# Eleven groups of one gate pair with right factors at an offset or read in steps, and matmuls in another order or size

## The chip, the cores and the metric

One core of a Trainium2 chip runs the whole kernel. The metric is the device time of one execution in microseconds (us), lower is better; of several runs the median is taken. The engines named below are PE (TensorE, matrix products; PEld are its weight loads), DVE (VectorE), ACT (ScalarE), POOL (GpSimd) and SP (SyncE, whose queue issues most transfers).

## The reference

One layer of a decoder on 512 tokens of 2048 channels, in float32: a norm and a projection `h @ w_in`; two mixers side by side on its columns (chunked gated linear attention with 4 heads, dilated sliding-window attention with 8 heads); `x + concat @ w_out`; then the feed-forward part

```
h2 = rms_norm(x, norm2_g[l])
x = x + (jax.nn.silu(h2 @ w_gate[l]) * (h2 @ w_up[l])) @ w_down[l]
```

with 5632 hidden columns. The change touches only `h2 @ w_gate` and `h2 @ w_up` for the hidden columns 2048 to 2559.

## The kernel before

All large products go through `pair` (L221 to L327). It computes two 512-column blocks of a product, `w1` and `w2`, by a Strassen-like scheme with seven products, in the order P1, P5, P6, P3, P7, P2, P4 (`PRODUCTS`, L32). A product runs over the groups `g` of 512 rows of the contracted side (four in a gate pair), and writes two accumulators `dst[m]` of 128 x 512 in PSUM, one bank each. For a group it takes the left combination `op.t[COMBO[prod], g]` (tiles AA and AS, made long before) and a right factor `src` of 128 x 2 x 512, which is a loaded quarter (a, b, c, d: tiles wa, wb, wc, wd; `load_quarter`, L215 to L219) or a difference of two quarters formed in place on DVE (L280, L283, L288, L293).

Float32 is carried in two parts in the matmul format `float32r`. ACT casts `src` to the high part wh (L295), DVE subtracts to get the low part wl (L297), and PE does 12 matmuls of 128 x 128 by 128 x 512 (L305): the high part with both parts of the left factor (eight), then the low part with its high part (four). The inner loop is

```
for w, terms in ((wh, (0, 1)), (wl, (0,))):
    for jj in range(2):
        for m in range(2):
            for hl in terms:
```

so that two matmuls in a row go to the same bank for wh, and every matmul changes bank for wl. wh and wl each have two buffers (`hpool`, L114), the quarters twelve (`wpool`, L113). After a group `step()` (L445) lets pieces of other work in: here, in the first groups of a gate pair, the transposes and stores of the pair before (L1014 to L1029) and the sums over its result (`sums_job`, L1305). When a product is complete its accumulators are copied to seeds by ACT (L243) or added to them by DVE (L255).

Eleven gate pairs (j = 0 to 10, L1348) run one after the other; the fifth has j = 4. Only the first `pair`-like function, `first_pair`, has its order of instructions on PE, ACT and DVE written by hand; after it the framework's planner orders the instructions of each engine when the program is built, gives out the buffers of a pool and adds the waits. P1.2 below is product P1, group 2 (groups count from 0).

Of the kernel before, what the change touches and what calls it, by code (L numbers as in the profile page):

```python
# [10 lines left out]
F32 = mybir.dt.float32  # L11
F32R = mybir.dt.float32r
U32 = mybir.dt.uint32
AF = mybir.ActivationFunctionType
ALU = mybir.AluOpType
# [3 lines left out]
P = 128  # L19
# [14 lines left out]
COMBO = {"P1": "A11", "P5": "S1", "P6": "S2", "P3": "S4", "P7": "S3", "P2": "A12", "P4": "A22"}  # L34
# [32 lines left out]
    "seedd",  # L67
    "closeb",
)
ON_VECTOR = "l1 u2 u4 u6 u7".split()  # L70


# [32 lines left out]
def block_kernel(ctx: ExitStack, tc: tile.TileContext, ins, out):  # L105
    nc = tc.nc
    x, w_in, w_out, w_gate, w_up, w_down = (
        ins[n] for n in ("x", "w_in", "w_out", "w_gate", "w_up", "w_down")
    )
# [3 lines left out]
    wpool = ctx.enter_context(tc.tile_pool(name="wpool", bufs=12))  # L113
    hpool = ctx.enter_context(tc.tile_pool(name="hpool", bufs=2))  # L114
# [10 lines left out]
    def nm(s):  # L125
        uid[0] += 1
        return f"{s}_{uid[0]}"
# [87 lines left out]
    def load_quarter(rows, name, g, w):  # L215
        r0 = rows[g][0 if name in "ab" else 1]
        t = wpool.tile([P, 2, 512], F32, name=nm("w" + name), tag="w")
        load(t, w[r0 : r0 + 256, :].rearrange("(j p) n -> p j n", p=P))
        return t  # L219

    def pair(op, rows, w1, w2, final, step, seed_scale=None):  # L221

        n = op.groups
        tt = nc.vector.tensor_tensor
        q = {}

        def quarter(name, g):
            if (name, g) not in q:
                q[name, g] = load_quarter(rows, name, g, w1 if name in "ac" else w2)
            return q[name, g]  # L230

        def accs():
            return [acc.tile([P, 512], F32, name=nm("acc"), tag="acc") for _ in range(2)]

        def seeds(src, half):
            res = []

            def one(m):
                t = cpool.tile([P, 512], F32, name=nm("seed"), tag="C")
                if seed_scale is None:  # L240
                    nc.scalar.copy(t, src[m])
                else:
                    nc.scalar.activation(t, src[m], AF.Copy, scale=seed_scale(half, m))  # L243
                res.append(t)

            later(1, lambda: one(0))
            later(2, lambda: one(1))
            return res

        def close(seed, src, half, which):  # L250
            def one(m):
                if seed_scale is None:
                    tt(seed[m], src[m], seed[m], op=ALU.add)
                else:
                    nc.vector.scalar_tensor_tensor(  # L255
                        seed[m], src[m], seed_scale(half, m), seed[m], op0=ALU.mult, op1=ALU.add
                    )
                if m == 1:
                    final(half, which, seed, None)

            later(1, lambda: one(0))
            later(2, lambda: one(1))

        X, Y, Z = None, None, None
        sa = sb = sc = None
        for prod in PRODUCTS:
            if prod == "P1":
                X = accs()
            elif prod == "P5":
                Y = accs()  # L270
            elif prod == "P2":
                Z = accs()
            dst = {"P1": X, "P5": Y, "P6": X, "P3": Y, "P7": X, "P2": Z, "P4": X}[prod]
            fresh = prod in ("P1", "P5", "P2")
            for g in range(n):
                if prod == "P1":
                    src = quarter("a", g)
                elif prod == "P5":
                    src = quarter("a", g)
                    tt(src, quarter("b", g), src, op=ALU.subtract)  # L280
                elif prod == "P6":
                    src = quarter("a", g)
                    tt(src, quarter("d", g), src, op=ALU.subtract)  # L283
                elif prod == "P3":
                    src = quarter("d", g)
                elif prod == "P7":
                    src = quarter("b", g)
                    tt(src, quarter("d", g), src, op=ALU.subtract)  # L288
                elif prod == "P2":
                    src = quarter("c", g)  # L290
                else:
                    src = quarter("a", g)
                    tt(src, quarter("c", g), src, op=ALU.subtract)  # L293
                wh = hpool.tile([P, 2, 512], F32R, name=nm("wh"), tag="wh")
                recent["act"] = nc.scalar.copy(wh, src).ins  # L295
                wl = hpool.tile([P, 2, 512], F32R, name=nm("wl"), tag="wl")
                tt(wl, src, wh.bitcast(F32), op=ALU.subtract)  # L297
                a = op.t[COMBO[prod], g]
                for w, terms in ((wh, (0, 1)), (wl, (0,))):
                    for jj in range(2):  # L300
                        for m in range(2):
                            for hl in terms:
                                first = g == 0 and w is wh and jj == 0 and hl == 0
                                last = g == n - 1 and w is wl and jj == 1
                                nc.tensor.matmul(  # L305
                                    dst[m],
                                    a[:, jj, hl, m * P : (m + 1) * P],
                                    w[:, jj, :],
                                    start=fresh and first,
                                    stop=last,  # L310
                                    skip_group_check=not fresh,
                                )
                step()
            if prod == "P1":
                sa = seeds(X, 0)
            elif prod == "P5":
                sb = seeds(Y, 1)
            elif prod == "P6":
                sc = seeds(X, 0)
            elif prod == "P3":  # L320
                close(sc, Y, 0, 1)
            elif prod == "P7":
                close(sb, X, 1, 1)
            elif prod == "P2":
                close(sa, Z, 0, 0)
            else:
                later(1, lambda: final(1, 0, None, X), hold=True)  # L327
# [113 lines left out]
    def later(units, fn, hold=False):  # L441

        deferred.append([units, fn, hold])

    def step(n=1):  # L445
        for d in list(deferred):
            d[0] -= 1
            if d[0] <= 0:
                deferred.remove(d)
                d[1]()  # L450
        if any(d[2] for d in deferred):
            return
        for _ in range(n):
            while background:
                try:
                    next(background[0])
                    break
                except StopIteration:
                    background.pop(0)
# [9 lines left out]
    def paced(counts):  # L469
        counts = iter(counts)  # L470
        return lambda: step(next(counts, 1))
# [113 lines left out]
    def x_turn(h, b, on_vector):  # L585
        bk = bank().rearrange("p (j n) -> p j n", j=2)
        for jj in range(2):
            for m in range(2):
                nc.tensor.transpose(
                    bk[:, jj, m * P : (m + 1) * P],  # L590
                    xt[h, b // 2][:, b % 2, m, jj * P : (jj + 1) * P],
                    ident,
                )
        dst = raw[b, h]
        if on_vector:
            nc.vector.tensor_tensor(
                dst, bk, g1[:, 2 * b : 2 * b + 2].unsqueeze(2).to_broadcast([P, 2, 256]), op=ALU.mult
            )
        else:
            for jj in range(2):  # L600
                nc.scalar.activation(
                    dst[:, jj, :], bk[:, jj, :], AF.Copy, scale=g1[:, 2 * b + jj : 2 * b + jj + 1]
                )
# [5 lines left out]
    for what in LOADS.split():  # L609
        name, i = what[0], int(what[1])  # L610
# [5 lines left out]
    for g in range(4):  # L616
        for b in (2 * g, 2 * g + 1):
            if g < 3:
                t = apool.tile([P, 2, 512], F32, name=nm("xT"), tag="A")
# [6 lines left out]
    def first_unit(what, *args):  # L626

        if what == "t":
            x_turn("ul".index(args[0][0]), int(args[0][1]), args[0] in ON_VECTOR)
            return  # L630
# [717 lines left out]
    for j in range(11):  # L1348
        c = slice(512 * j, 512 * j + 512)
        if j == 10:  # L1350
            background.append(down_jobs(0))
        pair(
            opn, rows_n, w_gate[:, c], w_up[:, c], final_ffn(j),
            paced(paces.get(j, ())), seed_scale=tok_scale,
        )


# [65 lines left out]
```

## Time and profile before

| | us |
|---|---|
| median of 3 runs (2046.26 to 2049.46) | 2046.87 |
| the profiled execution, its own time | 2051.18 |
| its span, first to last instruction | 2049.4 |
| PE busy | 2014.3 (98%) |
| DVE busy | 1659.6 (81%) |
| ACT busy | 1103.8 (54%) |

The page of the profile gives busy time by engine, the chain of work that ended last, and the costliest groups of instructions by line. Its times are those of one profiled execution, so a sum made from them stands against 2051.18 us, and the difference is then put on the median. A matmul's recorded duration is longer than the distance to the next one, since matmuls overlap; the pace is read from starts. Windows give busy times of a stretch, and the timeline gives instructions in order of time, neighbours of one kind merged ("x8").

### The profile page before, as it was taken

To read this page: it belongs to the slowest core of one execution; us is meant where nothing else is said; L and a number is where in the kernel's file an instruction comes from. 1 tells how busy PE (TensorE), PEld (TensorE's weight loads), DVE (VectorE), ACT (ScalarE), POOL (GpSimd) and SP (SyncE) were. 2 spreads that over 40 slices of the span, in tenths; PEclk is the share of its full clock that TensorE was granted. 3 is DMA by queue.
4 is the path that set the end of the run, shared out by engine and by line. 5 is a ranking of instruction groups with operands and counts; after the bars stand their busy time and mean duration, and the time that the engine had idled before them with its cause. 6 is when DMAs were issued, how large, how long until landed. Compare 5 with 4: busy or idle time off the path is not lost.

```text
span 2049.4 us, 25841 instructions
## 1 busy us (share of the span) xinstructions
PE 2014.3 (98%) x9226; PEld 1663.1 (81%) x9226; DVE 1659.6 (81%) x1850; ACT 1103.8 (54%) x1600; POOL 52.8 (3%) x81
## 2 busy tenths in 40 slices
PE   7999999999999999999999999999999999999999
PEld 6887888887777778888888888888888888888887
DVE  7996777768689789868868868778779979979977
ACT  7663564566666675544544445445446645545443
POOL 0000220011000000000000000000000000000000
PEclk9999999999999999999999999999999999999999
DMA  8347354454666685553554553553555855855662
GB/s 267 128 157 248 116 180 147 141 153 156 198 208 219 191 274 163 159 170 123 170 157 126 169 158 118 166 161 125 163 155 171 268 198 174 299 172 174 235 205 72
DMA packets 237114, 360.45 MB, mean 176 GB/s; under 512 B 18246, under 2 KB 96783, under 8 KB 236984
## 3 DMA queue, kind: packets, MB, share of 16 engines
q1 hardware_dynamic: 236776, 358.72, 55.5%
q8 instruction: 72, 1.18, 0.2%
q14 instruction: 58, 0.48, 0.1%
q10 hardware_dynamic: 208, 0.08, 0.0%
HBM read 296.59 MB, written 64.51 MB: 176 GB/s over the span
## 4 chain that ended last, share of the span: by engine, by line
PE 87%; DMA 5%; DVE 4%; issue 2%; ACT 1%; SPq 1%; POOL 0%; DVEq 0%; ACTq 0%; POOLq 0%
PE acc L305 79%; PE acc L373 3%; DVE wl L297 2%; PE bank L1014 1%; PE bank L921 1%; DMA wc<-in_w_in 1%; DMA xn_d<-oT 1%; PE bank L899 1%; DMA x<-in_x 1%; ACT wh L295 0%; DVE wa L283 0%; DMA r<-xn_d 0%; DVE AS L172 0%; PE bank L914 0%; PE bank L696 0%
## 5 line engine op out<-in xcount | busy, mean ns | idle before, releaser
L305 PE MATMUL acc<-wh,AS 128*128 128x512 f32 x3008 | 753.4, 392 | 3.6 <-ACT wh L295 2.2
L305 PEld LDWEIGHTS acc<-wh,AS 128*128 128x128 f32 x3008 | 563.5, 188 | 124.3 <-ACT wh L295 3.7
L295 ACT CAST wh<-wa 128x1024 fp32r<-128x1024 f32 x376 | 396.0, 1054 | 438.4 <-PE acc L305 382.4
L305 PE MATMUL acc<-wh,AA 128*128 128x512 f32 x2256 | 565.4, 393 | 0.0
L297 DVE TENSOR_TENSOR wl<-wa,wh 128x1024 fp32r<-128x1024 f32 x376 | 459.1, 1222 | 104.3 <-ACT wh L295 99.7
L305 PEld LDWEIGHTS acc<-wh,AA 128*128 128x128 f32 x2256 | 422.2, 188 | 87.7 <-issue 1.2
L305 PE MATMUL acc<-wl,AS 128*128 128x512 f32 x1504 | 403.8, 390 | 3.0 <-DVE wl L297 3.0
L305 PEld LDWEIGHTS acc<-wl,AS 128*128 128x128 f32 x1504 | 282.4, 188 | 63.7 <-DVE wl L297 5.3
L305 PE MATMUL acc<-wl,AA 128*128 128x512 f32 x1128 | 302.5, 390 | 1.5 <-DVE wl L297 1.3
L305 PEld LDWEIGHTS acc<-wl,AA 128*128 128x128 f32 x1128 | 211.4, 188 | 47.2 <-DVE wl L297 3.5
L295 ACT CAST wh<-wb 128x1024 fp32r<-128x1024 f32 x94 | 99.0, 1054 | 126.1 <-PE acc L305 122.8
L295 ACT CAST wh<-wc 128x1024 fp32r<-128x1024 f32 x94 | 98.9, 1053 | 123.2 <-PE acc L305 111.5
L295 ACT CAST wh<-wd 128x1024 fp32r<-128x1024 f32 x94 | 99.1, 1055 | 114.5 <-PE acc L305 114.5
L297 DVE TENSOR_TENSOR wl<-wd,wh 128x1024 fp32r<-128x1024 f32 x94 | 114.9, 1223 | 51.2 <-ACT wh L295 51.0
L297 DVE TENSOR_TENSOR wl<-wc,wh 128x1024 fp32r<-128x1024 f32 x94 | 114.9, 1223 | 50.5 <-ACT wh L295 50.1
L293 DVE TENSOR_TENSOR wa<-wc,wa 128x1024 f32<-128x1024 f32 x94 | 114.8, 1225 | 43.7 <-DMA wc<-in_w_gate 25.8
L297 DVE TENSOR_TENSOR wl<-wb,wh 128x1024 fp32r<-128x1024 f32 x94 | 114.6, 1221 | 9.6 <-ACT wh L295 9.3
L288 DVE TENSOR_TENSOR wb<-wd,wb 128x1024 f32<-128x1024 f32 x94 | 115.0, 1224 | 0.6
L283 DVE TENSOR_TENSOR wa<-wd,wa 128x1024 f32<-128x1024 f32 x94 | 114.3, 1222 | 0.2
L280 DVE TENSOR_TENSOR wa<-wb,wa 128x1024 f32<-128x1024 f32 x94 | 113.6, 1222 | 0.8
L255 DVE SCALAR_TENSOR_TENSOR seed<-acc,rs,seed 128x512 f32<-128x512 f32 x96 | 71.8, 748 | 30.9 <-PE acc L305 29.8
L243 ACT ACTIVATE seed<-acc,rs 128x512 f32<-128x512 f32 x96 | 60.8, 680 | 0.0
(286 smaller groups left out, 1370.6 us busy)
## 6 DMA issues: line engine op xcount, KB each, us to landing
wa<-in_w_gate SPq DMA_DIRECT2D x44, 512.0 KB, 4.2
wb<-in_w_up SPq DMA_DIRECT2D x44, 512.0 KB, 3.8
wd<-in_w_up SPq DMA_DIRECT2D x44, 512.0 KB, 4.0
wc<-in_w_gate SPq DMA_DIRECT2D x44, 512.0 KB, 3.6
wc<-in_w_in SPq DMA_DIRECT2D x28, 512.0 KB, 4.1
wa<-in_w_in SPq DMA_DIRECT2D x24, 512.0 KB, 4.9
wb<-in_w_in SPq DMA_DIRECT2D x24, 512.0 KB, 5.8
wd<-in_w_in SPq DMA_DIRECT2D x24, 512.0 KB, 5.9
```

The lines of the kernel that those rows point to most:

```text
L243: nc.scalar.activation(t, src[m], AF.Copy, scale=seed_scale(half, m))
L255: nc.vector.scalar_tensor_tensor(seed[m], src[m], seed_scale(half, m), seed[m], op0=ALU.mult, op1=ALU.add)
L280: tt(src, quarter("b", g), src, op=ALU.subtract)
L283: tt(src, quarter("d", g), src, op=ALU.subtract)
L288: tt(src, quarter("d", g), src, op=ALU.subtract)
L293: tt(src, quarter("c", g), src, op=ALU.subtract)
L295: recent["act"] = nc.scalar.copy(wh, src).ins
L297: tt(wl, src, wh.bitcast(F32), op=ALU.subtract)
L305: nc.tensor.matmul(dst[m], a[:, jj, hl, m * P : (m + 1) * P], w[:, jj, :], start=fresh and first, stop=last, skip_group_check=not fresh,)
L373: recent["pe"] = nc.tensor.matmul(dst[prod][m], a[:, jj, hl, m * P : (m + 1) * P], w[:, jj, :], start=fresh and g == 0 and len(terms) == 2 ...
L899: nc.tensor.matmul(lp[:, :n], qh[:, b * P : (b + 1) * P], kh[:, :n], start=True, stop=True)
L921: nc.tensor.matmul(op, vh[:, k, :], lgs[b][:, k * P : (k + 1) * P], start=(k == 0), stop=(k == b))
```

## The change

A table `FORMS` gives eleven groups of the pair j = 4 another form; `pair` gets it as an argument and, for these, calls the new `one_group` in place of its own cast, subtraction and matmuls.

- A number (P1.1: 1, P1.2: 4, P5.1: 8, P2.2: 16): the high part is cast, in two halves, into two tiles of the pool of the quarters, at an offset of so many elements. The low part is as before.
- `("read", b)` (P5.2: 2, P3.1: 4, P6.1: 16, P6.2: 256): both parts are written so that element k of a row comes to lie with its neighbour b elements further on, and are read back by the matmul with a step of b elements.
- `"same"` (P7.1): the high and the low right part follow each other on the same left factor.
- `"banks"` (P7.2): the matmuls change bank every time in the high part too.
- `"split"` (P2.1): each matmul becomes two of 256 columns.

In all eleven the low part is formed by two subtractions of 512 columns instead of one of 1024.

```diff
--- before.py
+++ after.py
@@ -67,6 +67,12 @@
     "seedd",
     "closeb",
 )
+
+FORMS = {
+    ("P1", 1): 1, ("P1", 2): 4, ("P5", 1): 8, ("P5", 2): ("read", 2), ("P6", 1): ("read", 16),
+    ("P6", 2): ("read", 256), ("P3", 1): ("read", 4), ("P7", 1): "same",
+    ("P7", 2): "banks", ("P2", 1): "split", ("P2", 2): 16,
+}
 ON_VECTOR = "l1 u2 u4 u6 u7".split()
 
 
@@ -218,7 +224,90 @@
         load(t, w[r0 : r0 + 256, :].rearrange("(j p) n -> p j n", p=P))
         return t
 
-    def pair(op, rows, w1, w2, final, step, seed_scale=None):
+    def spread(t, b):
+
+        return t.rearrange("p (a b) -> p b a", b=b)
+
+    def moving(form, src):
+
+        if isinstance(form, tuple):
+            b = form[1]
+            wh = hpool.tile([P, 2, 512], F32R, name=nm("wh"), tag="wh")
+            for jj in range(2):
+                nc.scalar.copy(
+                    spread(wh[:, jj], b), src[:, jj].rearrange("p (b a) -> p b a", b=b)
+                )
+            return [wh[:, 0], wh[:, 1]]
+        res = []
+        for jj in range(2):
+            t = wpool.tile([P, 2, 512], F32, name=nm("woff"), tag="w")
+            v = t.rearrange("p j n -> p (j n)").bitcast(F32R)[:, form : form + 512]
+            nc.scalar.copy(v, src[:, jj])
+            res.append(v)
+        return res
+
+    def one_group(form, src, dst, a):
+
+        tt = nc.vector.tensor_tensor
+
+        def mm(m, jj, hl, w, cols=None):
+            o, r = dst[m], w
+            if cols is not None:
+                o, r = o[:, cols], r[:, cols]
+            nc.tensor.matmul(
+                o, a[:, jj, hl, m * P : (m + 1) * P], r,
+                start=False, stop=False, skip_group_check=True,
+            )
+
+        def mv(m, jj, hl, w, o):
+            nc.tensor.matmul(
+                o, a[:, jj, hl, m * P : (m + 1) * P], w,
+                start=False, stop=False, skip_group_check=True,
+            )
+
+        if isinstance(form, (int, tuple)):
+            wh = moving(form, src)
+        else:
+            t = hpool.tile([P, 2, 512], F32R, name=nm("wh"), tag="wh")
+            nc.scalar.copy(t, src)
+            wh = [t[:, 0], t[:, 1]]
+        wl = hpool.tile([P, 2, 512], F32R, name=nm("wl"), tag="wl")
+        for jj in range(2):
+            if isinstance(form, tuple):
+                b = form[1]
+                o = spread(wl[:, jj], b)
+                x = src[:, jj].rearrange("p (b a) -> p b a", b=b)
+                y = spread(wh[jj].bitcast(F32), b)
+            else:
+                o, x, y = wl[:, jj], src[:, jj], wh[jj].bitcast(F32)
+            tt(o, x, y, op=ALU.subtract)
+        wl = [wl[:, 0], wl[:, 1]]
+        jm = [(jj, m) for jj in range(2) for m in range(2)]
+        if form == "same":
+            for jj, m in jm:
+                mm(m, jj, 0, wh[jj])
+                mm(m, jj, 0, wl[jj])
+            for jj, m in jm:
+                mm(m, jj, 1, wh[jj])
+            return
+        if form == "banks":
+            for w, terms in ((wh, (0, 1)), (wl, (0,))):
+                for hl in terms:
+                    for jj, m in jm:
+                        mm(m, jj, hl, w[jj])
+            return
+        for w, terms in ((wh, (0, 1)), (wl, (0,))):
+            for jj, m in jm:
+                for hl in terms:
+                    if form == "split":
+                        mm(m, jj, hl, w[jj], slice(0, 256))
+                        mm(m, jj, hl, w[jj], slice(256, 512))
+                    elif isinstance(form, tuple):
+                        mv(m, jj, hl, spread(w[jj], form[1]), dst[m])
+                    else:
+                        mm(m, jj, hl, w[jj])
+
+    def pair(op, rows, w1, w2, final, step, seed_scale=None, forms={}):
 
         n = op.groups
         tt = nc.vector.tensor_tensor
@@ -291,11 +380,15 @@
                 else:
                     src = quarter("a", g)
                     tt(src, quarter("c", g), src, op=ALU.subtract)
+                a = op.t[COMBO[prod], g]
+                if (prod, g) in forms:
+                    one_group(forms[prod, g], src, dst, a)
+                    step()
+                    continue
                 wh = hpool.tile([P, 2, 512], F32R, name=nm("wh"), tag="wh")
                 recent["act"] = nc.scalar.copy(wh, src).ins
                 wl = hpool.tile([P, 2, 512], F32R, name=nm("wl"), tag="wl")
                 tt(wl, src, wh.bitcast(F32), op=ALU.subtract)
-                a = op.t[COMBO[prod], g]
                 for w, terms in ((wh, (0, 1)), (wl, (0,))):
                     for jj in range(2):
                         for m in range(2):
@@ -1352,6 +1445,7 @@
         pair(
             opn, rows_n, w_gate[:, c], w_up[:, c], final_ffn(j),
             paced(paces.get(j, ())), seed_scale=tok_scale,
+            forms=FORMS if j == 4 else {},
         )
 
 
```

## Rows read from the trace of the kernel before

**Rows 1.** The page: PE's busy time; the chain that ended last, by line
```profile
PE 2014.3 (98%) x9226; PEld 1663.1 (81%) x9226; DVE 1659.6 (81%) x1850; ACT 1103.8 (54%) x1600; POOL 52.8 (3%) x81
...
PE acc L305 79%; PE acc L373 3%; DVE wl L297 2%; PE bank L1014 1%; PE bank L921 1%; DMA wc<-in_w_in 1%; DMA xn_d<-oT 1%; PE bank L899 1%; DMA x<-in_x 1%; ACT wh L295 0%; DVE wa L283 0%; DMA r<-xn_d 0%; DVE AS L172 0%; PE bank L914 0%; PE bank L696 0%
```

**Rows 2.** Windows, fifth pair, P1's end, P5, P6, P4: busy us, PEclk, DMA
```profile
1079.40:1090.28 10.88, 10.88 (x54) 9.09 (x53) 10.88 (x11) 5.57 (x8) 0.00 (x0) 1.00 0.20 67
1090.28:1101.16 10.88, 10.88 (x50) 9.01 (x49) 10.77 (x13) 5.39 (x7) 0.00 (x0) 1.00 0.50 176
1101.16:1112.04 10.88, 10.88 (x50) 9.01 (x49) 6.83 (x6) 5.38 (x7) 0.00 (x0) 1.00 0.07 26
...
1144.68:1157.34 12.66, 12.66 (x61) 10.59 (x60) 10.22 (x11) 7.34 (x11) 0.00 (x0) 1.00 0.70 207
```

**Rows 3.** Timeline of PE, fifth pair: start us, us, engine, line, instruction
```profile
1086.67 1.03 PE L1014 MATMUL bank<-mats,seed 128*128 128x128 f32 x8
1087.46 2.07 PE L305 MATMUL acc<-wh,AA 128*128 128x512 f32 x8
...
1090.28 1.98 PE L305 MATMUL acc<-wh,AS 128*128 128x512 f32 x8
1092.09 1.07 PE L305 MATMUL acc<-wl,AS 128*128 128x512 f32 x4
1093.00 1.98 PE L305 MATMUL acc<-wh,AS 128*128 128x512 f32 x8
...
1125.64 1.98 PE L305 MATMUL acc<-wh,AS 128*128 128x512 f32 x8
...
1168.22 1.98 PE L305 MATMUL acc<-wh,AS 128*128 128x512 f32 x8
```

**Rows 4.** Groups of instructions, fifth pair: busy us, mean ns, idle before
```profile
L305 PEld LDWEIGHTS acc<-wh,AS 128*128 128x128 f32 x128 | 24.0, 188 | 5.0
L297 DVE TENSOR_TENSOR wl<-wa,wh 128x1024 fp32r<-128x1024 f32 x17 | 20.8, 1222 | 5.3 <-ACT wh L295 5.3
...
L295 ACT CAST wh<-wa 128x1024 fp32r<-128x1024 f32 x16 | 16.9, 1055 | 20.7 <-PE acc L305 19.0 <-DVE wl L297 1.7
```

**Rows 5.** PE's float32 products of the attention: groups by shape, and timeline
```profile
L899 PE MATMUL bank<-k,q 128*128 128x512 f32 x8 | 4.1, 594 | 0.0
...
449.61 1.02 PE L899 MATMUL bank<-k,q 128*128 128x512 f32 x2
```

**Rows 6.** Timeline of PE, the small gate projection and what follows it
```profile
61.32 2.04 PE L696 MATMUL bank<-AS,gs 128*128 128x256 f32 x16
63.20 1.09 PE L373 MATMUL acc<-wl,AS 128*128 128x512 f32 x4
```

**Rows 7.** Timeline of DVE, fifth pair; in brackets the idle time before
```profile
1090.35 1.22 DVE L283 TENSOR_TENSOR wa<-wd,wa 128x1024 f32<-128x1024 f32 x1
...
1097.44 1.22 DVE L297 TENSOR_TENSOR wl<-wa,wh 128x1024 fp32r<-128x1024 f32 x1
...
1117.34 1.22 DVE L293 TENSOR_TENSOR wa<-wc,wa 128x1024 f32<-128x1024 f32 x1 [0.46 <-DMA wc<-in_w_gate]
...
1123.47 1.23 DVE L293 TENSOR_TENSOR wa<-wc,wa 128x1024 f32<-128x1024 f32 x1 [0.63 <-DMA wc<-in_w_gate]
...
1125.27 1.22 DVE L297 TENSOR_TENSOR wl<-wb,wh 128x1024 fp32r<-128x1024 f32 x1
```

**Rows 8.** Groups by shape: a cast and a subtraction of 512 columns
```profile
L171 ACT CAST AS<-xT 128x512 fp32r<-128x512 f32 x16 | 9.7, 616 | 0.0
...
L172 DVE TENSOR_TENSOR AS<-xT,AS 128x512 fp32r<-128x512 f32 x16 | 10.8, 687 | 0.0
```

**Rows 9.** SP's queue, loads for the fifth pair; issues, median us to landing
```profile
1054.76 8.53 SPq L218 DMA_DIRECT2D wb<-in_w_up  x4
1065.64 8.58 SPq L218 DMA_DIRECT2D wd<-in_w_up  x4
...
wd<-in_w_up SPq DMA_DIRECT2D x44, 512.0 KB, 4.0
```

## The prediction

> **What bounds the kernel now.** I read the page's busy shares and its chain first. PE is busy 98% of the span, and 79% of the chain that ended last are the product matmuls of line 305 [rows 1]. So an edit costs what it adds to PE's stream, or what it makes PE wait. [...]
>
> PE's timeline gives the pace. Group P5.0 (product P5, group 0) starts at 1090.28, its four low matmuls at 1092.09, the next group at 1093.00, the next pair's P5.0 at 1168.22 [rows 3]: 1.81/8 = 0.226 us from start to start for the high eight, 0.91/4 = 0.227 for the low four, 2.72 us a group, 77.94 us a pair. The eight visit each bank twice in a row, the four change bank at every matmul, and the pace is one: the order of banks costs nothing. Weight loads, 188 ns each, fill 9.0 of 10.88 us [rows 4, 2] and hide.
>
> **The change, part by part.** No matmul goes except that 12 become 24; no weight DMA is added.
>
> Offsets (P1.1, P1.2, P5.1, P2.2: four groups): the eight high matmuls of each read 512 contiguous words from word 1, 4, 8 or 16 of a buffer. Nothing in the trace starts there. Lower end 0, the row of 0.227; upper end for all eight of one group 8 × (0.432 − 0.227) = 1.6 us, by the slowest columns below. I take 0: the words are still neighbours.
>
> Steps (P5.2 at 2; P3.1 at 4; P6.1 at 16; P6.2 at 256): both factors are written spread out and read with that step, 12 matmuls each. This is the one large term, and no row shows PE reading its right factor in steps. The lower end is 0. For the upper side I take the rows in which PE takes 512 columns most slowly at full clock, the plain float32 ones of line 899: two cover 1.02 us and one lasts 0.594 [rows 5], so the second starts 0.43 us after the first, 0.205 us more than a product matmul. Further out lies the weight load: 128 columns in 188 ns make 0.752 for 512, 0.525 more; that is a record's length, not a pace, since eight transposes, a load each, take only 1087.46 − 1086.67 = 0.79 us [rows 3]. For steps of 4, 16 and 256, whose words lie apart, I take the float32 row: 36 × 0.205 = 7.4 us. The step of 2 uses half of what it passes, so I put it midway between the contiguous row and the slow one: 12 × 0.10 = 1.2 us (0 to 2.5).
>
> [...]
>
> Halves (P2.1): 24 matmuls of 256 columns. The small gate projection has such ones: 16 from 61.32 to 63.20 [rows 6], 0.118 us each with a weight load each. 24 × 0.118 = 2.82 against 2.72: +0.1 us. If the load's 0.188 were the pace it would be 4.5, or +1.8; the row says otherwise.
>
> Order (P7.1 "same", P7.2 "banks"): banks, nothing, as shown. "Same" wants the low factor at its second matmul, not its ninth. P7.1 starts on PE at 1125.64 [rows 3]; its low factor runs on DVE from 1125.27 to 1126.49, with a subtraction at 1123.47 before it that waited 0.63 us for a load [rows 7]. It is now made in halves, the first ready at about 1125.96 where PE wants it at 1125.87, the second at about 1126.65 where it wants it at about 1126.55. So +0.2 us, 0 to 0.6. The high buffer is also held four matmuls, 0.9 us, longer; the cast two groups on starts that much later, takes 1.05, and PE wants it 2.72 us after its new start.
>
> ACT and DVE: in all eleven groups the low factor becomes two subtractions of 512 columns, 2 × 0.687 = 1.37 for 1.22; in the eight with an offset or a step the cast becomes two, 2 × 0.616 = 1.23 for 1.05 [rows 8, 4]. That is 11 × 0.15 = 1.7 and 8 × 0.18 = 1.4 us, nothing on PE's path while DVE stays ahead. It is tightest at P5.3: the low factor ends at 1097.44 + 1.22 = 1098.66 [rows 7], and PE wants it 1.81 us into the group that starts at 1093.00 + 2 × 2.72, at 1100.25: 1.6 us of cover, and the four changed groups before it take 0.6. If stepped words cost DVE double, P5.2 takes another 1.4, and some 0.4 us shows on PE.
>
> Buffers: each offset group borrows two of the twelve weight buffers until PE has read them. The loads of b wait for a buffer from 1054.76 on, those of d from 1065.64 [rows 9]; d is wanted for P6's first subtraction at 1090.35 [rows 7]. A buffer lent to P1.1 comes back at about 1084, to P1.2 at 1087, and a load lands 4.0 us after its issue [rows 9]. So the last of d comes close to its use; where it is late, the subtraction holds DVE's queue behind it, and SP's queue holds the sum job's loads and stores behind a load without a buffer. I take 0, at most one landing, 4.0 us.
>
> The engines' order: after the first pair it comes from the framework's planner, for P4's subtraction (L293) already runs at 1117.34, in P3 [rows 7]. Other instructions can swap places from this pair on; as PE has no gap to lose or gain there, nothing, ±0.5.
>
> **Sum**: 7.4 + 1.2 + 0.1 + 0.2 = 8.9 us. The profiled execution took 2051.18 us (its span 2049.4 and 1.8 around it), which makes 2060.1; it stands 4.3 us above the median of the runs, 2046.87, and against that median the forecast is **2055.8**.
>
> **The rivals.** *Steps are free on PE.* Only 0.1 + 0.2 is left: 2047.2, not slower. For it: the float32 rows may be slow for their arithmetic, and then say nothing of reading. Against it: PE takes a word every (0.227 − 0.118)/256 = 0.43 ns, the fastest reading in this trace, and so has the least room for words that lie apart. It decides if P6.1 takes 2.72 us. Chance 0.27.
>
> *Steps cost more than half the pace.* If a far word takes what a column takes in a weight load, 36 × 0.525 + 12 × 0.205 + 0.3 = 21.7 us: 2068.6; midway between the two prices, about 2063. For it: nothing in the trace bounds it; against it: no row has a pace this slow. Chance 0.20.
>
> *A load comes late.* With free steps and a buffer lent too long, PE waits up to one landing: +4.3, 2051.2. For it: DVE waits for each wc as it is (0.46 and 0.63 us) [rows 7]; against it: none of that reaches PE. Chance 0.05.
>
> *It gains.* Weights used twice in a row could need one load. 16 matmuls repeat one; even if all took no time, that is 3.6 us, and their loads are hidden. Chance 0.02, half of it large enough to count.
>
> **How the numbers follow.** A measurement of this kernel can tell 0.2%, 4.1 us, from no change. The forecast, steps at about half pace, has 0.46 and its own range 2053.5 to 2058.5 (step 2 from free to full price, DVE's 0.4, the planner). The range for all goes from the free case less what the runs scatter, 2046.3 (the lowest run took 2046.26), into the dearer case up to 2066.0, which is a price of (19.1 − 2.8)/36 = 0.45 us a matmul, and leaves out one in ten. Slower: 0.46 + 0.20 + most of 0.05 = 0.70; same 0.29; faster 0.01.
>
> **What would show it.** In the changed profile PE's start-to-start in P6.1, P6.2 and P3.1 should be about 0.43 us and those groups 5.2 us long, P5.2 between 2.7 and 5.2; offsets and "banks" at 0.227; halves at 0.118. The extra time should lie in this pair, its 77.94 us becoming about 86.8, with no more idle time on PE. I am wrong if the stepped groups keep 2.72 us, if they pass 7, or if the time lies in PE's waits for a factor or in a late load.

## The result, and the profile after

The changed kernel takes **2056.86 us** (median of 4 runs, 2055.8 to 2058.47); the kernel before, run beside it, 2047.3 (2046.26 to 2049.46). The ratio is 1.0042, with an interval of 1.003 to 1.0054, so it is slower by 6 to 11 us, beyond the 0.2% that can be told from no change. The profiled execution took 2055.8 us, its span 2054.0, at a mean granted clock of 0.998.

The page of the changed kernel, PE's busy time and the chain by line (what `pair` did in L305 is now L398; L257 and L263 are the two matmul calls of `one_group`, L263 the one that reads in steps):

```profile
PE 2021.1 (98%) x9238; PEld 1662.5 (81%) x9238; DVE 1663.0 (81%) x1861; ACT 1105.7 (54%) x1608; POOL 53.8 (3%) x81
...
PE acc L398 80%; PE acc L466 3%; PE bank L1107 1%; DVE wl L391 1%; PE acc L257 1%; PE acc L263 1%; PE bank L1014 1%; PE bank L992 1%; DMA wc<-in_w_in 1%; DMA x<-in_x 1%; DMA xn_d<-oT 1%; DMA r<-xn_d 0%; DVE wa L372 0%; PE bank L1007 0%; DVE
```

PE has 12 instructions more, the halves, and 6.8 us more busy time than in [rows 1]; the chain is still PE's. The share of the stepped line, 1%, is a whole chain's rounding; what it costs is read from the pair.

PE's timeline of the changed kernel, fifth pair (start us, us, engine, line, instruction):

```profile
1086.33 1.98 PE L398 MATMUL acc<-wh,AS 128*128 128x512 f32 x8
...
1089.05 2.03 PE L257 MATMUL acc<-woff,AS 128*128 128x512 f32 x8
...
1091.85 3.78 PE L263 MATMUL acc<-wh,AS 128*128 128x512 f32 x8
...
1097.27 2.01 PE L398 MATMUL acc<-wh,AS 128*128 128x512 f32 x8
...
1102.74 3.63 PE L263 MATMUL acc<-wh,AS 128*128 128x512 f32 x8
...
1107.92 1.91 PE L263 MATMUL acc<-wh,AS 128*128 128x512 f32 x8
1109.67 1.03 PE L263 MATMUL acc<-wl,AS 128*128 128x512 f32 x4
1110.53 1.99 PE L398 MATMUL acc<-wh,AS 128*128 128x512 f32 x8
...
1115.99 3.84 PE L263 MATMUL acc<-wh,AS 128*128 128x512 f32 x8
...
1121.49 2.03 PE L398 MATMUL acc<-wh,AS 128*128 128x512 f32 x8
...
1124.28 1.98 PE L398 MATMUL acc<-wh,AS 128*128 128x512 f32 x8
...
1172.55 1.75 PE L398 MATMUL acc<-wh,AS 128*128 128x512 f32 x7
```

Read it by starts, as in [rows 3]. From P5.0 to the next pair's P5.0 it is now 1172.55 − 1086.33 = 86.22 us, against 77.946 before rounding (77.94 in [rows 3]): **+8.27 in this one pair**. The step of 2 (P5.2) fills 1091.85 to 1097.27, 5.42 us in place of 2.72. The step of 16 (P6.1) fills 1102.74 to 1107.92, 5.18. The step of 256 (P6.2), right behind it, needs 1107.92 to 1110.53, **2.61: less than a plain group**, 0.216 us a matmul. The step of 4 (P3.1) takes 1115.99 to 1121.49, 5.50. A group at an offset (P5.1, from 1089.05) takes 2.80.

Windows of the same kernel over P5 and P6 (from to, us; busy us and instructions of PE, PEld, DVE, ACT, POOL; PEclk, DMA share, GB/s):

```profile
1086.33:1100.02 13.69, 13.69 (x49) 9.24 (x48) 10.98 (x14) 4.50 (x7) 0.00 (x0) 1.00 0.62 209
1100.02:1113.27 13.25, 13.25 (x49) 9.24 (x48) 10.79 (x11) 7.23 (x9) 0.00 (x0) 1.00 0.11 41
```

PE has no gap in either and its clock is 1.00, as in [rows 2]. Its weight loads fill 9.2 us, about as before (9.0). So the added time is not a wait: it lies inside the matmuls that read in steps. DVE, which filled all of P5 before, now has 2.7 us to spare there, since PE is the slower one.

DVE's timeline of the changed kernel, low parts written with a step (x2 are two of 512 columns):

```profile
1090.08 1.29 DVE L283 TENSOR_TENSOR wl<-wa,wh 128x512 fp32r<-128x512 f32 x2
...
1101.04 2.11 DVE L283 TENSOR_TENSOR wl<-wa,wh 128x512 fp32r<-128x512 f32 x2
```

and ACT's, the high parts:

```profile
1085.67 1.21 ACT L237 CAST wh<-wa 128x512 fp32r<-128x512 f32 x2 [1.19 <-issue]
...
1102.29 2.16 ACT L237 CAST wh<-wa 128x512 fp32r<-128x512 f32 x2
```

The first DVE row and the first ACT row are the step of 2, 0.69 and 0.66 us each, near the price of contiguous words (0.687 and 0.616 in [rows 8]). The second rows are the steps of 16 (DVE) and 256 (ACT), 1.11 and 1.19 us each, at nearly twice that. DVE's rows both write in that step and read wh in it; ACT's only write in it. None of it reaches PE, which is busy throughout.

### The profile page after: what moved, and what is told of

The parts are those of the page before. It is cut to its first block, busy times and chain, and to the rows that moved or that the text cites. A ratio compares the mean times of both kernels' runs of the same rounds, so it can differ in the third digit from the quotient of the medians.

```text
span 2054.0 us, 25874 instructions
## 1 busy us (share of the span) xinstructions
PE 2021.1 (98%) x9238; PEld 1662.5 (81%) x9238; DVE 1663.0 (81%) x1861; ACT 1105.7 (54%) x1608; POOL 53.8 (3%) x81
## 3 DMA queue, kind: packets, MB, share of 16 engines
q8 instruction: 72, 1.18, 0.2%
## 4 chain that ended last, share of the span: by engine, by line
PE 90%; DVE 4%; DMA 3%; issue 1%; SPq 1%; ACT 1%; POOL 0%; DVEq 0%; ACTq 0%; POOLq 0%
PE acc L398 80%; PE acc L466 3%; PE bank L1107 1%; DVE wl L391 1%; PE acc L257 1%; PE acc L263 1%; PE bank L1014 1%; PE bank L992 1%; DMA wc<-in_w_in 1%; DMA x<-in_x 1%; DMA xn_d<-oT 1%; DMA r<-xn_d 0%; DVE wa L372 0%; PE bank L1007 0%; DVE AS L178 0%
## 5 line engine op out<-in xcount | busy, mean ns | idle before, releaser
L398 PE MATMUL acc<-wh,AS 128*128 128x512 f32 x2952 | 740.0, 392 | 4.8 <-ACT wh L389 3.4
L398 PEld LDWEIGHTS acc<-wh,AS 128*128 128x128 f32 x2952 | 553.1, 188 | 124.6 <-ACT wh L389 5.8
L389 ACT CAST wh<-wa 128x1024 fp32r<-128x1024 f32 x370 | 389.6, 1054 | 439.2 <-PE acc L398 381.3
L398 PE MATMUL acc<-wh,AA 128*128 128x512 f32 x2224 | 556.0, 392 | 0.0
L391 DVE TENSOR_TENSOR wl<-wa,wh 128x1024 fp32r<-128x1024 f32 x370 | 451.2, 1221 | 106.2 <-ACT wh L389 97.2
L398 PEld LDWEIGHTS acc<-wh,AA 128*128 128x128 f32 x2224 | 415.0, 188 | 86.2 <-issue 1.0
L398 PE MATMUL acc<-wl,AS 128*128 128x512 f32 x1476 | 396.1, 390 | 3.2 <-DVE wl L391 3.2
L398 PEld LDWEIGHTS acc<-wl,AS 128*128 128x128 f32 x1476 | 276.9, 188 | 63.1 <-DVE wl L391 5.5
L398 PE MATMUL acc<-wl,AA 128*128 128x512 f32 x1112 | 298.3, 390 | 1.7 <-DVE wl L391 1.7
L398 PEld LDWEIGHTS acc<-wl,AA 128*128 128x128 f32 x1112 | 208.3, 188 | 46.9 <-DVE wl L391 3.8
```

The source lines that it names most:

```text
L398: nc.tensor.matmul(dst[m], a[:, jj, hl, m * P : (m + 1) * P], w[:, jj, :], start=fresh and first, stop=last, skip_group_check=not fresh,)
```

## The experiments

In all of them the groups of one pair are set by a table like the change's `FORMS`, and a pace is the time from one matmul's start to the next, so that a smaller one is faster. A figure is the mean of a group, or, where its first matmuls differ, of those behind them.

**1. Which distance is it?** Steps of 4 and 16 double the pace, 256 does not. The theories for that are in the expectation. Here the right factor is read from *two* places in turn, word by word, 2 to 128 words apart ("pair"), and with more steps ("read"). A "pair" of 1 is the plain order in this form.

```diff
...
+        ("P1", 1): ("pair", 128), ("P1", 2): ("pair", 64), ("P5", 1): ("pair", 32),
+        ("P5", 2): ("pair", 16), ("P6", 1): ("pair", 8), ("P6", 2): ("pair", 4),
+        ("P3", 1): ("pair", 2), ("P3", 2): ("read", 256), ("P7", 1): ("read", 128),
+        ("P7", 2): ("read", 64), ("P2", 1): ("read", 32), ("P2", 2): ("read", 8),
+        ("P4", 1): ("pair", 1),
...
+        if f[0] == "pair":
+            return t.rearrange("p (n t k) -> p n k t", t=2, k=f[1])
```

> Thirteen groups of the fifth pair, each with another way of reading: pairs of neighbouring columns lie 1, 2, 4, 8, 16, 32, 64 or 128 words apart and the next pair one word on (form pair), or all columns are read with a step of 8, 32, 64, 128 or 256 words (form read). Start to start of PE's matmuls, us. Theory A (the two words of a pair must lie far enough apart, in another part of the memory, to be fetched together): pair 1 at 0.227; pair 2, 4, 8, 16 near 0.43 to 0.46 as steps 2, 4 and 16 were; from some distance between 32 and 256 words on 0.216, and the steps of the same length alike: read 8 at 0.43 or more, read 128 and 256 at 0.216. [...] Theory C (an innermost count of two is a case of its own): every pair from 2 on at 0.216, every read but 256 at 0.43 or more.

One run: 2061.63 us, the kernel before 2049.25 beside it. PE's timeline (pair 128 and its low part; pair 4 and its low part; pair 2; read 128 and its low part; read 64 and its low part):

```profile
1080.56 1.89 PE L274 MATMUL acc<-wh,AA 128*128 128x512 f32 x8
1082.28 1.03 PE L274 MATMUL acc<-wl,AA 128*128 128x512 f32 x4
...
1107.29 1.89 PE L274 MATMUL acc<-wh,AS 128*128 128x512 f32 x8
1109.01 1.16 PE L274 MATMUL acc<-wl,AS 128*128 128x512 f32 x4
...
1115.52 1.98 PE L274 MATMUL acc<-wh,AS 128*128 128x512 f32 x8
...
1126.30 2.40 PE L274 MATMUL acc<-wh,AS 128*128 128x512 f32 x8
1128.53 1.30 PE L274 MATMUL acc<-wl,AS 128*128 128x512 f32 x4
1129.67 4.16 PE L274 MATMUL acc<-wh,AS 128*128 128x512 f32 x8
1133.64 2.13 PE L274 MATMUL acc<-wl,AS 128*128 128x512 f32 x4
```

From 1080.56 to 1082.28 are eight matmuls: 0.215 us. Pairs 128, 64, 32, 16, 8 and 4 words apart all run at 0.216, pair 2 and plain at 0.227. Theory A, the distance, falls: the pace goes with how many places are visited before the reading comes back. Two places, 0.216; four (read 128), 0.283; eight (read 64), **0.487**, the slowest row of all; 16 and 64 places (read 32, read 8) 0.433 and 0.431. The pair 2 words apart visits two places as well and has no gain (0.227), so two words apart is too near here and four is far enough (three was not run). A step of 256 words is two places, and ran at the pace of the pairs in the change too (0.216). Theory C fails at pair 2 and read 128 alone. Why the pace goes with the places, no run shows.

The groups at 0.216 in P5 and P6 did not make that stretch quicker. A window of it (columns as above):

```profile
1100.00:1110.00 10.00, 9.20 (x41) 7.57 (x41) 10.00 (x11) 6.94 (x8) 0.00 (x0) 1.00 0.20 79
```

DVE is full for these 10 us and PE stands idle for 0.8: with subtractions that write spread-out words (1.1 to 1.2 us for 512 columns at steps of 4, 16 and 256 in the change), DVE is the bound here as soon as PE is faster. That matters in experiment 6.

**2. What do the offsets cost?** The four groups at an offset took 2.78 to 2.81 us, not 2.72. Either the borrowed buffer is to blame, or the offset. Here right factors lie in borrowed buffers at words 0, 2, 32 and 64, and in other groups the *left* factor is copied to words 0, 1, 4, 16, 64 and 256 of one.

```diff
...
+        ("P1", 1): 0, ("P1", 2): 2, ("P5", 1): 32, ("P5", 2): 64, ("P7", 1): ("left", 0),
+        ("P7", 2): ("left", 1), ("P2", 1): ("left", 4), ("P2", 2): ("left", 16), ("P4", 1): ("left", 64),
+        ("P4", 2): ("left", 256),
```

> Ten groups of the fifth pair with offsets alone: the high right factor from word 0, 2, 32 and 64 of a buffer, and the left factor copied to word 0, 1, 4, 16, 64 and 256 of one. Theory D (in the change the offsets themselves cost, 0.231 to 0.236 for 0.227): word 0 at 0.227, word 2 at 0.231 to 0.236; words 32 and 64 at either. Rival E (it is the group's form, its buffers or what runs beside it, and not the offset): word 0 too at 0.231 or more. For the 0.011 us by which a contiguous matmul is slower than the one with the step of 256: rival F (the weight load's reads meet the right factor's, by the place of the two in memory) expects the pace to move with the left factor's offset by more than 0.004 us between the six; without F all six are at 0.227.

One run: 2055.15 us against 2049.25. PE's timeline (right factor at word 0, at word 2; two rows for further down; left factor at word 1, at word 4):

```profile
1077.85 1.98 PE L259 MATMUL acc<-woff,AA 128*128 128x512 f32 x8
...
1080.57 2.04 PE L259 MATMUL acc<-woff,AA 128*128 128x512 f32 x8
...
1107.19 1.70 PE L417 MATMUL acc<-wl,AS 128*128 128x512 f32 x4 [1.84 <-DVE wl L410]
1108.69 3.12 PE L417 MATMUL acc<-wh,AS 128*128 128x512 f32 x8
...
1131.61 2.02 PE L259 MATMUL acc<-wh,aoff 128*128 128x512 f32 x8
...
1139.86 1.98 PE L259 MATMUL acc<-wh,aoff 128*128 128x512 f32 x8
```

A borrowed buffer at word 0 keeps 0.227, so it is the offset itself, as theory D has it: word 2 gives 0.235, word 32 0.232, word 64 again 0.227. The left factor moves the same matmuls, as rival F has it: at words 0, 4, 64 and 256 they take 0.227, at 1 and 16 0.2325 and 0.233, though PE stands idle for none of its loads there. The plain pace thus moves with the place of either factor; what happens when both are moved was not run, and that the two reads meet, as rival F puts it, was not shown. The place is not all either: in the changed kernel P3.2, a plain group behind the step of 4, takes 2.79 us (1121.49 to 1124.28), with single matmuls at 0.224 to 0.236 behind its first before they settle at 0.227. The groups with the left factor at word 1 or 16 do not settle within their twelve.

So the left factor's place costs up to 0.006 us a matmul here. The weight loads change too beside a slower read: in the changed kernel those of the groups with steps of 2 and 16 last 0.202 us on the mean in the high part and 0.206 to 0.208 in the low one, in place of 0.188 [rows 4], and those of the step of 256 0.189 to 0.191.

This kernel also showed the rival "a load comes late". Two groups of P1 and two of P5 borrow eight buffers here, and the loads behind them are late: SP issues the last of b at 1085.94 and those of d from 1090.85 on, where the kernel before issues d from 1065.64 on [rows 9]. DVE's timeline has waits of 1.29 us for wb (at 1089.85), 1.34 for a load of the sum job (at 1093.02) and 1.58 for wd (at 1104.77); the third and fourth row above are PE's behind the last of them. Its windows there:

```profile
1098.00:1107.20 9.20, 5.24 (x22) 3.61 (x21) 7.45 (x8) 4.20 (x5) 0.00 (x0) 1.00 0.58 200
1107.20:1110.20 3.00, 3.00 (x8) 2.36 (x9) 3.00 (x3) 1.04 (x1) 0.00 (x0) 0.58 0.00 0
```

PE stands idle for 3.96 of 9.20 us, and in the next 3 us its granted clock averages 0.58, where the row before has 1.00: the twelve matmuls from 1107.19 take 4.46 us (to 1111.65) in place of 2.72. The pair grows to 84.66 us: of the 6.7 added, 3.96 are PE's waits and 1.74 the slower matmuls behind them, of which the lower clock makes an estimated 3 × (1 − 0.58) = 1.26. So the late loads cost nearly half as much again here as the waits, 1.74 on 3.96.

**3. and 4. Is it these three groups and nothing else?** One kernel leaves the steps of 2, 16 and 4 out of the change, the other keeps only them.

```diff
...
-    ("P1", 1): 1, ("P1", 2): 4, ("P5", 1): 8, ("P5", 2): ("read", 2), ("P6", 1): ("read", 16),
-    ("P6", 2): ("read", 256), ("P3", 1): ("read", 4), ("P7", 1): "same",
-    ("P7", 2): "banks", ("P2", 1): "split", ("P2", 2): 16,
+    4: {
+        ("P1", 1): 1, ("P1", 2): 4, ("P5", 1): 8, ("P6", 2): ("read", 256), ("P7", 1): "same",
+        ("P7", 2): "banks", ("P2", 1): "split", ("P2", 2): 16,
```

> The change without its three groups P5.2, P6.1 and P3.1 (steps of 2, 16 and 4); the other eight forms stay. Theory (these three carry the whole loss, 12 x (0.225 + 0.207 + 0.233) = 8.0 us by their paces): 2047.3 + 0.3 = 2047.6, within 0.1% of before, and the next pair's P5 starts 78.2 us after this one's. Rival (part of the 9.6 us between the medians comes from the borrowed buffers or another order of the instructions): 2048.8 or more, and PE idle in or behind the fifth pair.

```diff
...
+    ("P5", 2): ("read", 2), ("P6", 1): ("read", 16), ("P3", 1): ("read", 4),
```

> The change with its three groups P5.2, P6.1 and P3.1 alone (steps of 2, 16 and 4). Theory (they carry the loss): this pair's P5 to the next one's 77.95 + 12 x (0.225 + 0.207 + 0.233) = 85.9 us, and the ratio to before 1 + 8.0/2048 = 1.0039. Rival (the borrowed buffers, the two subtractions for one and the planner carry a part of it, as the median of the eight others, 2 us over before, could be read): 1.0030 or less.

Without the three: 2051.44 us (2048.93 to 2053.4, 10 runs) against 2049.25, ratio 1.0008 (0.9999 to 1.0018). With the three alone: 2056.58 (2055.56 to 2060.17, 5 runs) against 2048.59, ratio **1.0041** (1.0027 to 1.0055). PE's timeline, both ends of the pair, of the kernel without them:

```profile
1091.19 1.98 PE L399 MATMUL acc<-wh,AS 128*128 128x512 f32 x8
...
1169.37 1.98 PE L399 MATMUL acc<-wh,AS 128*128 128x512 f32 x8
```

and of the kernel with them alone:

```profile
1087.40 1.98 PE L396 MATMUL acc<-wh,AS 128*128 128x512 f32 x8
...
1173.41 1.98 PE L396 MATMUL acc<-wh,AS 128*128 128x512 f32 x8
```

78.19 us and 86.01 us, against 77.946: +0.24 and +8.07. The three groups are the loss. The ratios alone do not show it: the eight's median, 2.2 us over before, is where its rival put it (2048.8 or more), and the lower end of the three's interval, 1.0027, is within what its rival allowed (1.0030 or less). The traces decide. The period of the eight is 0.24 longer, and PE is not idle in or behind that pair, which the rival wanted: from 790 to 1990 us it is busy for all 1200. What makes the eight's median 2.2 us longer elsewhere is open; the ratio's interval includes no change.

**5. One place, or two?** A step of 2 uses two words of every four and costs as much as a step of 16 (0.452 and 0.433 us a matmul in the change). Is it that the read moves on after too few words, or that the words are no neighbours? "run r, s" reads r neighbours, skips to the next multiple of s, and comes back for the rest. A later pair (j = 6) puts offsets on the step of 256 and on plain groups.

```diff
...
+        ("P1", 1): (("run", 2, 4), 0, 0), ("P1", 2): (("run", 4, 8), 0, 0),
+        ("P5", 1): (("run", 2, 256), 0, 0), ("P5", 2): (("run", 4, 256), 0, 0),
...
+        if f[0] == "run":
+            return t.rearrange("p (n k r) -> p k n r", k=f[2] // f[1], r=f[1])
```

> Runs of neighbouring words: run r, s reads r contiguous words, then the r words s further on, to the end of the row, then sweeps again. Fifth pair: run 2,4; 4,8; 4,16; 8,64; 2,8; 2,256; 4,256; 2,128; step 2 again; step 256 again; plain. [...] Seventh pair: step 256 with the right factor from word 1 and 16, and with the left factor from word 1 and 16; plain with the left factor from word 1, 2, 8 and 32. [...] Rival (each offset costs by itself): the four with step 256 are 0.004 or more above 0.216.

One run: 2062.82 us against 2048.59. PE's timeline (run 2, 4 and its low part; run 4, 8 and its low part; then in the other pair step 256 with the left factor at word 1, and plain with the left factor at word 1):

```profile
1080.20 3.78 PE L286 MATMUL acc<-wh,AA 128*128 128x512 f32 x8
1083.80 1.99 PE L286 MATMUL acc<-wl,AA 128*128 128x512 f32 x4
1085.62 2.04 PE L286 MATMUL acc<-wh,AA 128*128 128x512 f32 x8
1087.50 1.10 PE L286 MATMUL acc<-wl,AA 128*128 128x512 f32 x4
...
1293.30 1.89 PE L286 MATMUL acc<-wh,aoff 128*128 128x512 f32 x8
1295.03 1.03 PE L286 MATMUL acc<-wl,aoff 128*128 128x512 f32 x4
...
1303.96 2.02 PE L286 MATMUL acc<-wh,aoff 128*128 128x512 f32 x8
1305.82 1.08 PE L286 MATMUL acc<-wl,aoff 128*128 128x512 f32 x4
```

| read | us a matmul |
|---|---|
| plain | 0.227 |
| 4 of every 8 words; 4 of every 16; 8 of every 64 | 0.235, 0.225, 0.233 |
| 2 of every 4; 2 of every 8; 2 of every 128 | 0.451, 0.461, 0.445 |
| every 2nd word (again) | 0.452 |
| 2 of every 256; 4 of every 256 | 0.338, 0.25 |
| every 256th (again) | 0.216 |

In a read that moves on through the row, **two neighbours a visit are as dear as one** (0.445 to 0.461 beside 0.452), and four or eight are near plain (0.225 to 0.235). 4 of every 256, which stay with two places, take 0.25. Visits of four neighbours or more thus ran near the plain pace here, those of two every 4, 8 or 128 words at about half of it, as single words did at steps of 2 to 64 (0.43 to 0.49); three, and four that begin elsewhere than at a multiple of four, were not run. Open is the step of 256 beside "2 of every 256": both stay with two places, and the one that changes place at every word is faster, 0.216 to 0.338. So is why eight places (0.487) are dearer than 64 (0.431).

ACT and DVE price these forms otherwise where they write them (DVE reads wh in them too): the step of 2 takes 0.66 and 0.69 us for 512 columns in the change, near the contiguous 0.616 and 0.687 [rows 8], and two of every 4, 8, 128 or 256 words take 0.65 to 0.70 in this run, while steps of 4, 16 and 256 take 1.1 to 1.2 in the change. For PE's reads two words a visit cost as much as one (0.451 for two of every 4, 0.452 for every 2nd), and the fastest read of all, 0.216, changes place at every word.

The last rows tell the offsets' story further: a plain group with its left factor at word 1 takes 0.2325, a group with the step of 256 takes 0.216 with either factor at word 0, 1 or 16. The reading from two places is faster *and* does not feel the left factor's place.

**6. A version that beats both.** If any read from two places runs at 0.216, a plainly written factor can be read so: the tile stays as it is, the matmul takes words 0, 256, 1, 257, ..., the accumulator's columns come out in that order, and ACT and DVE put them back as they read PSUM. All products of `pair` and `first_pair` do this; no write is spread, so DVE's subtraction keeps its price.

```diff
+    def turns(t):
+        return t.rearrange("p (b a) -> p a b", b=2)
+    def halves(t):
+        return t.rearrange("p (b a) -> p b a", b=2)
+    def back(t):
+        return t.rearrange("p (a b) -> p b a", b=2)
...
-                    nc.scalar.activation(t, src[m], AF.Copy, scale=seed_scale(half, m))
+                    nc.scalar.activation(
+                        halves(t), back(src[m]), AF.Copy, scale=seed_scale(half, m)
+                    )
...
-                                    w[:, jj, :],
+                                    turns(w[:, jj, :]),
```

> The kernel before with every right factor of the large products read in pairs 256 words apart straight from its tile, nothing written in steps; the products' columns then stand in pairs in PSUM, and ACT and DVE read them back with a step of two words where they copy, close or use an accumulator. Theory (the pace of 0.216 is a property of that way of reading, whatever wrote the tile): 8232 matmuls x 0.0109 = 90 us less, 1957 us, or up to 1975 where DVE, full in P1 and P5, or a load becomes what PE waits for. Rival G (the step-256 group was fast because of its place or what ran beside it): 2047. Rival H (reading PSUM in steps of two words doubles the evacuations and these reach PE): pace 0.216, but PE idle at the ends of products, over 1975.

**1985.04 us** (1983.7 to 1985.58, 4 runs) against 2049.25: ratio **0.9683** (0.9669 to 0.9698), 64 us less, though 10 more than the slower end of what was expected. Its page, PE's busy time:

```profile
PE 1930.9 (97%) x9226; PEld 1671.3 (84%) x9226; DVE 1655.8 (83%) x1850; ACT 1098.0 (55%) x1600; POOL 55.2 (3%) x81
```

Its PE timeline:

```profile
1101.18 1.89 PE L320 MATMUL acc<-wh,AA 128*128 128x512 f32 x8
...
1103.77 1.89 PE L320 MATMUL acc<-wh,AA 128*128 128x512 f32 x8
```

A group is 2.59 us, and most gate pairs 74.27 where they were 77.95: the pace belongs to the way of reading, and rival G falls. The time lies where rival H put it, over 1975, but its cause, that ACT and DVE read PSUM at half speed in steps of two words, falls. The two groups that copy and add accumulators, in this kernel:

```profile
L255 ACT ACTIVATE seed<-acc,rs 128x512 f32<-128x512 f32 x96 | 60.9, 683 | 0.0
...
L269 DVE SCALAR_TENSOR_TENSOR seed<-acc,rs,seed 128x512 f32<-128x512 f32 x96 | 71.6, 746 | 23.8 <-PE acc L320 23.8
```

683 and 746 ns; the kernel before has 680 and 748. What is short of the expected gain shows in the waits (us in total, times, longest), here of this kernel:

```profile
PE acc L320 <- DVE wl L312: 14.8, 18, 1.7
```

and of the kernel before:

```profile
PE acc L305 <- DVE wl L297: 4.3, 6, 1.3
```

PE's busy time fell by 83.4 us (2014.3 to 1930.9), its idle time grew by 17.3, from 35.1 to 52.4 of the span. Two windows of this kernel:

```profile
550.00:790.00 240.00, 221.36 (x1029) 186.69 (x1028) 212.65 (x243) 159.64 (x251) 6.93 (x7) 0.98 0.65 212
790.00:1580.00 790.00, 788.05 (x3733) 689.69 (x3732) 654.93 (x645) 410.36 (x473) 0.00 (x0) 1.00 0.53 168
```

and the kernel before, over nearly the same work as in the first:

```profile
557.00:810.00 253.00, 240.27 (x1090) 194.43 (x1089) 222.42 (x261) 168.41 (x265) 6.75 (x7) 0.99 0.67 214
```

In the second, which holds most of the gate pairs, PE keeps nearly all of the gain. In the first DVE is busy for 89% of the time and PE stands idle for 18.6 us; but in the kernel before it stood idle there for 12.7 already, so this stretch has about 6 of the 17.3 us. The rest is spread: counted between the same matmuls, about 5 us ahead of it, 2 in the gate pairs and 4 behind them. Most of the added wait is for DVE: PE waits for the low part 18 times in place of 6, 10.5 us more, and DVE has 9% of the chain in place of 4%. A third buffer for wl, which might even that out, was not tried.

## Why the prediction was right, and where its steps were not

The forecast, 2055.8 us and slower, holds: 2056.86. By its own steps:

| step | forecast, us | in the trace, us |
|---|---|---|
| step of 4 | +2.46 | +2.78 |
| step of 16 | +2.46 | +2.46 |
| step of 256 | +2.46 | **−0.11** |
| step of 2 | +1.2 | **+2.70** |
| offsets, four groups | 0 | +0.31 |
| halves (P2.1) | +0.1 | +0.15 |
| same (P7.1) | +0.2 | 0 |
| banks (P7.2) | 0 | 0 |
| sum | 8.9 | 8.3 |

With 0.01 to 0.06 us more in each plain group behind a changed one, the pair's own 8.4 is complete (8.27 from P5.0, 0.14 in P1). The two profiled executions differ by only 4.6 us, because that of the changed kernel reaches P5.0 of this pair 3.95 us sooner (1086.33 against 1090.28); the medians differ by 9.6, the ratio's interval means 6 to 11.

- *The bound.* Right: PE has no gap before [rows 2] or after (13.69 of 13.69 us and 13.25 of 13.25), so the cost is what the edits add to its stream.
- *The price of a far word.* The float32 rows' 0.43 us [rows 5] was taken as nearest, and 0.433 and 0.460 were measured for 16 and 4. That the two agree does not show a common cause: the slowest read, 0.487, passes it.
- *The step of 256 was put among "words that lie apart".* This is a wrong step, worth 2.6 us, and by the prediction's own sign ("wrong if the stepped groups keep 2.72 us") it failed here, at 2.61. Its words lie furthest apart and are read fastest, as are the pairs of experiment 1, word by word from two places (0.216).
- *The step of 2 "midway".* Also wrong, by 1.5 us, and outside its 0 to 2.5: two words of every four are no better than one (0.452 and 0.460 us a matmul in the change; experiment 5). This error and the one before it have opposite signs and nearly cancel, 2.6 against 1.5; with the 0.3 of the offsets and the 0.3 of the step of 4 the sum came out 0.6 above the pair's trace. The total was met partly by luck.
- *Offsets at 0* because "the words are still neighbours": they cost 0.06 to 0.09 us a group (experiment 2), small here.
- *"Same"*: the low factor was in time; the group keeps 2.72 us, and nothing of the 0.2 shows. PE, later by then, starts it at 1129.72, and DVE has made both halves by 1128.93. The price was also misread by one matmul: the second half is wanted at the sixth, 1126.77 by the old starts, and not at 1126.55. *Halves*: 0.120 us each where the row gave 0.118.
- *ACT and DVE.* That stepped words could cost DVE double was named for P5.2; the step of 2 is the one that keeps 0.69 us for 512 columns on DVE, and the steps of 16, 256 and 4 take 1.10 to 1.18. The cover held, for PE itself had become slower.
- *A load comes late.* It did not decide here; DVE's waits for wc stay at 1.5 us at most, behind PE's longer groups. It did in experiment 2, where P5.2 borrows buffers too: 3.96 us of waiting, over several loads and close to the 4.0 priced for one, and 1.74 more behind it, an estimated 1.26 of it by the clock, which the rival's price left out.
- *Steps are free*, *more than half pace*: the first is out by P6.1's 5.18 us, the second by its 0.433 a matmul; neither is wholly false, as 256 takes 0.216 and 64 costs 0.487 (experiment 1).

## What to carry to other kernels

Price the right factor's access pattern by how many neighbours a read takes in a visit and how many places it returns to. In float32r, with 512 columns, reads of four or eight neighbours a visit took 0.225 to 0.235 us a matmul here and reads in turn from two places 4 to 256 words apart 0.216, while single words at steps of 2 to 64, and two neighbours every 4, 8 or 128 words, took about twice the plain 0.227, 0.43 to 0.49. PE being the bound here, reading words 0, 256, 1, 257, ... and undoing it at the evacuation of PSUM gave 3.2% of this kernel without one more instruction. Then look at once at the engine that feeds PE, for part of the gain goes into its waits: PE's busy time fell by 83.4 us here, and its idle time grew by 17.3.

## What was not expected of the hardware

- A plain read of 512 neighbouring words, 0.227 us, is not the fastest: word by word from two places, 4 to 256 words apart, it is 0.216.
- The pace of a plain matmul moves with the place of its *left* factor, 0.227 to 0.233, and with the right one's, 0.227 to 0.236; the read from two places 256 words apart feels neither.
- Eight places are slower than 16 or 64: 0.487 against 0.433 and 0.431. No run explains it.
- ACT and DVE read PSUM with a step of two words at the plain price (683 and 746 ns); writing SBUF with a step of 4, 16 or 256 words costs them nearly double (1.1 to 1.2 us for 512 columns, where contiguous words take 0.616 and 0.687), a step of 2 little or nothing (0.66 and 0.69).
